# Hybrid attention/mLSTM block on one core: the low parts of the mixers' weight pieces and the rotary swap given to adding DMAs

## The chip, the cores and the metric

The kernel runs on one core of a Trainium2 chip. The metric is the device time of one execution in microseconds (us). Five engines matter: TensorE (PE in the profile, with its weight loads as PEld), VectorE (DVE), ScalarE (ACT), GpSimd (POOL) and SyncE (SP), which issues the loads from HBM.

## The reference, cut to what matters

Two layers, each a mixer and a convolutional feed-forward part, on 512 tokens of 1024 features, all in float32:

```
for l in range(2):
    mixed = hybrid_mixer(rms_norm(x), w_in[l], ..., w_out[l])    # attention heads | mLSTM heads
    x = x + rms_norm(mixed)
    ff = conv_ffn(rms_norm(x), w_up[l], ..., w_down[l])
    x = x + rms_norm(ff)

def apply_rotary(t):               # per head, 64 features
    t1, t2 = t[..., :32], t[..., 32:]
    return concatenate([t1 * cos - t2 * sin, t2 * cos + t1 * sin], axis=-1)
```

`hybrid_mixer` projects the normed input by `w_in` to queries and keys of the attention (rotated as above), values, the mLSTM's queries, keys and values, an output gate and the mLSTM's gates; it runs dilated window attention over 8 heads and an mLSTM in both directions over 4 heads, and multiplies the joined result by `w_out`.

## The kernel before, in words

**Precision.** Every weight tile and every activation is split in a high part (rounded to float32r) and a low part, the remainder. `mac` makes a product of three matmuls: high weight by high activation (line 230), low weight by high activation (231), high weight by low activation (232). The projection of values, in which the weights are the moving operand, does the same in lines 923 to 925.

**Pieces.** `plan` lists the weights in the order of use, in pieces of 128 x 1024 numbers (512 KB): per layer 28 of `w_in` (numbers 0 to 27 of the layer), 8 of `w_out`, 44 of `w_up` and 24 of `w_down`, 104 in all. SP loads a piece into one of three `wraw` buffers. `split_w` makes the parts: ScalarE copies the piece to `whi` (line 183), then VectorE subtracts that from the piece into `wlo` (`lo_part`, line 115), and the load of a later piece is issued, which waits until its `wraw` buffer is free. `whi` and `wlo` have three buffers each, so a piece can be split when the matmuls of the piece three before it are done. `prefetch` keeps two pieces split ahead of the one in use.

**The mixer's order.** `ORDER` names the pieces of four rounds: q and k are the mLSTM's projections, V the two pieces of the values (of both the mLSTM and the attention), a and b the attention's queries and keys of two heads. After the rounds come four pieces (m) of the output gate.

```
ORDER = ["qkaVb", "aqbkV", "qkVab", "qabkV"]
```

Between the steps of a projection the generators `attn` (stream A) and `mlstm` (stream M) are pumped: each `yield` in them ends one small share of work, and a rate says how many shares go with one step. The work of `attn(r)` is started when a, b and V of its round are done, and `A.run()` finishes it before the next a or b is rotated.

**The rotation.** `rot_out` takes the projection `ps` in PSUM (128 features: two heads of two halves of 32). Four ScalarE copies of 32 partitions (line 707) put the halves, swapped in pairs, into `b`; VectorE multiplies `ps` by the cosines (708), `b` by the sines with their signs (709) and adds (710). Then ScalarE and VectorE make high and low parts of the heads (lines 713 to 723 and `lo_part`).

**Who sets the order.** Every engine runs its own list in order. The lists are laid out by a planner from the program order, the dependences and its own estimates of how long each operation takes; an operation that the planner takes to be ready may stand ahead of one that comes earlier in the program.

Of the kernel before, what the change touches and what calls it, by code (L numbers as in the profile page):

```python
# [11 lines left out]
AF = mybir.ActivationFunctionType  # L12
ALU = mybir.AluOpType
# [12 lines left out]
RAW = 3  # L26
LINE = 256
RING = 3
HD = 128
KSC = HD ** -0.5  # L30
SUM1, ROW1, SUM2, ROW2 = [int(t * 2400) for t in (0.6, 3.3, 2, 8)]
# [50 lines left out]
def tile_hybrid_block(ctx: ExitStack, tc: tile.TileContext, xt, w_in, w_g, w_out, w_up, w_down, par, cst, out):  # L82
    nc = tc.nc
# [30 lines left out]
    def lo_part(dst, src, hi):  # L114
        nc.vector.tensor_tensor(out=dst, in0=src, in1=f32v(hi), op=ALU.subtract)  # L115
# [50 lines left out]
    def split_w(alloc=None):  # L166

        if not raw_q:
            return None
        raw, nk, i = raw_q.popleft()  # L170
        parts = {}
        n = 8
        k = 0
        while k < nk:
            if alloc is None:

                o = 16 if i in moving else 0
                hi, lo = (q.tile([P, 8 * P + LINE // 4], F32R, tag=t, name=t)[:, o:o + 8 * P].rearrange("p (k c) -> p k c", k=8)
                          for q, t in ((whi_p, "whi"), (wlo_p, "wlo")))
            else:  # L180
                hi, lo, n = alloc()
            m = min(n, nk - k)
            nc.scalar.copy(out=hi[:, 0:m, :], in_=raw[:, k:k + m, :])  # L183
            lo_part(lo[:, 0:m, :], raw[:, k:k + m, :], hi[:, 0:m, :])
            for j in range(m):
                parts[k + j] = (hi[:, j, :], lo[:, j, :])
            parts["all"] = (hi, lo)
            k += m
        load_raw()
        return parts  # L190
# [320 lines left out]
    def mixer(l, xp, first, mp, post):  # L511
# [7 lines left out]
        cosr, sinr, biasT, rowmask = cc("cos", T), cc("sin", T), cc("bias", 896), cc("rowmask", 8)  # L519
# [10 lines left out]
        gps, pss, scale, more = first  # L530
# [171 lines left out]
        def rot_out(ps, name):  # L702
            a = mp.tile([P, T], F32, tag="ca", bufs=2, name="ra")
            b = mp.tile([P, T], F32, tag="cu", bufs=2, name="rb")
            for q in range(4):
                o_ = 32 * (q ^ 1)
                nc.scalar.copy(out=b[32 * q:32 * q + 32, :], in_=ps[o_:o_ + 32, :])  # L707
            nc.vector.tensor_tensor(out=a, in0=ps, in1=cosr, op=ALU.mult)
            nc.vector.tensor_tensor(out=b, in0=b, in1=sinr, op=ALU.mult)
            nc.vector.tensor_tensor(out=a, in0=a, in1=b, op=ALU.add)  # L710
            A_, B_ = slice(0, 64), slice(64, 128)
            t = [mp.tile([P, T], F32R, tag=name + i, name=name + i) for i in "01"]
            nc.scalar.copy(out=t[0][A_], in_=a[A_])
            nc.scalar.copy(out=t[1][B_], in_=a[B_])
            if name == "aq":

                lo_part(t[0][B_], a[A_], t[0][A_])
                lo_part(t[1][A_], a[B_], t[1][B_])
                st[name] = t
            else:  # L720

                nc.scalar.copy(out=t[0][B_], in_=f32v(t[0][A_]))
                nc.scalar.copy(out=t[1][A_], in_=f32v(t[1][B_]))
                lo_part(klo[0][A_], a[A_], t[0][A_])
                lo_part(klo[1][B_], a[B_], t[1][B_])
                st[name] = (t, klo)
# [9 lines left out]
        def attn(hp):  # L736
            qs2, (kh, kl) = st["aq"], st["ak"]
            ct = new_cat(hp)

            def scores(a, qt):  # L740
                qs = slice(qt * P, (qt + 1) * P)
                s = s_ps()
                nc.tensor.matmul(out=s, lhsT=qs2[a][:, qs], rhs=kh[a], start=True, stop=False)  # L743
                nc.tensor.matmul(out=s, lhsT=qs2[a][:, qs], rhs=kl[a], start=False, stop=True)
                p_ = mp.tile([P, T], F32, tag="p", bufs=2, name="p")
                mx = sm.tile([P, 1], F32, tag="mx", bufs=4, name="mx")

                o_ = 384 - qt * P
                nc.vector.tensor_tensor_reduce(out=p_, in0=s, in1=biasT[:, o_:o_ + T], scale=-0.125, scalar=3e38,  # L749
                                               op0=ALU.add, op1=ALU.min, accum_out=mx)  # L750
                den = sm.tile([P, 1], F32, tag="den", bufs=4, name="den")
                nc.scalar.activation(out=p_, in_=p_, func=AF.Exp, scale=-1.0, bias=mx, accum_out=den)  # L752
                nc.vector.reciprocal(out=den, in_=den)
                nc.scalar.activation(out=p_, in_=p_, func=AF.Copy, scale=den)
                return p_

            def turn(p_, pt, qi):
                tp = t_ps()
                for kk in range(4):
                    nc.tensor.transpose(tp[:, kk * P:(kk + 1) * P], p_[:, kk * P:(kk + 1) * P], ident)  # L760
                tv = tp.rearrange("p (k q) -> p k q", k=4)
                hi = pt[0][:, :, qi * P:(qi + 1) * P]
                nc.scalar.copy(out=hi, in_=tv)
                lo_part(pt[1][:, :, qi * P:(qi + 1) * P], tv, hi)

            units = [(a, qt) for a in range(2) for qt in range(4)]
            held = scores(*units[0])
            yield
            for n, (a, qt) in enumerate(units):
                cur = held  # L770
                if n + 1 < len(units):
                    held = scores(*units[n + 1])
                    yield
                if qt % 2 == 0:
                    pt = (mp.tile([P, 4, 2 * P], F32R, tag="pth", bufs=2, name="pth"),
                          mp.tile([P, 4, 2 * P], F32R, tag="ptl", bufs=2, name="ptl"))
                turn(cur, pt, qt % 2)
                yield
                if qt % 2 == 1:
                    if qt == 1:  # L780
                        o = o_ps()
                    ov = o[:, (qt - 1) * P:(qt + 1) * P]
                    vs = st["av"]
                    for i in range(2):
                        for kk in range(4):
                            nc.tensor.matmul(out=ov, lhsT=vs[:, kk, a].rearrange("p i e -> p (i e)"), rhs=pt[i][:, kk, :],  # L786
                                             start=(i == 0 and kk == 0), stop=(i == 1 and kk == 3))
                    if qt == 3:
                        c = ct[64 * a:64 * a + 64, :]
                        nc.scalar.copy(out=c, in_=o[64:128, :])  # L790
                        nc.vector.tensor_tensor(out=c, in0=o[0:64, :], in1=c, op=ALU.add)
                    yield
# [96 lines left out]

        prefetch(RING - 1)  # L890
        scale_ready()
# [40 lines left out]
        for r in range(4):  # L932
            done = set()
            for c in ORDER[r]:
# [7 lines left out]
                else:  # L942
                    ps = proj()
# [10 lines left out]
        for r in range(4):  # L954
            ps = proj()
# [59 lines left out]
        for m in range(G, KT - 2):  # L1015
            w = take()
            ps = o_ps() if m == G else mm_ps()
# [167 lines left out]
def _constants():  # L1185
    import numpy as np

    f = np.float32
    c = np.zeros((P, NCC), f)

    def put(name, a):
        c[:, CC[name]:CC[name] + a.shape[1]] = a

    i = np.arange(P)
    put("ident", np.eye(P, dtype=f))
    put("tri_f", (i[:, None] <= i[None, :]).astype(f))
    put("tri_b", (i[:, None] >= i[None, :]).astype(f))
    put("mask_f", np.where(i[:, None] <= i[None, :], 0.0, -1e30).astype(f))
    put("mask_b", np.where(i[:, None] >= i[None, :], 0.0, -1e30).astype(f))
    rm = np.zeros((P, 8), f)  # L1200
    ic = np.zeros((P, 4), f)
    for part in range(4):
        for d in range(2):
            for j in range(4):
                for h in range(4):
                    r = part * 32 + d * 16 + j * 4 + h
                    rm[r, d * 4 + h] = 1.0
                    ic[r, j if d == 0 else 3 - j] = 1.0
    put("rowmask", rm)
    put("ind", ic)  # L1210
    put("dir", (i[:, None] // 16 % 2 == np.arange(2)).astype(f))
    dh = 64
    inv = (f(10000.0) ** (-np.arange(0, dh, 2, dtype=f) / f(dh))).astype(f)
    ang = np.arange(T, dtype=f)[:, None] * inv[None, :]
    cos, sin = np.cos(ang).astype(f).T, np.sin(ang).astype(f).T
    put("cos", np.concatenate([cos, cos, cos, cos]))
    put("sin", np.concatenate([-sin, sin, -sin, sin]))

    off = (np.arange(896)[None, :] - 384) - i[:, None]
    a = np.abs(off)  # L1220
    n = (a <= 64).astype(int) + ((a % 4 == 0) & (a <= 256)) + ((a % 16 == 0) & (a <= 1024))
    put("bias", np.where(n > 0, 8.0 * np.log(np.maximum(n, 1)), -1e30).astype(f))
    return c
# [58 lines left out]
```

## Time and profile before

| | |
|---|---|
| median of 3 runs | 1354.69 us (1354.68 to 1354.85) |
| the profiled execution | 1353.89 us, of which the span from the first to the last instruction is 1352.0 us |
| mean granted TensorE clock | 0.996 of full speed |
| busy, share of the span | TensorE 98%, VectorE 71%, ScalarE 53%, GpSimd 6% |
| DMA | 115.34 MB, mean 85 GB/s; the load queue takes 27.9% of the 16 DMA engines' time |

Stages in the profiled execution: the first mixer's projections and streams run from about 24 to 262 us, the second mixer's from about 695 to 931 us; between and behind them lie the products with `w_out` and the feed-forward parts. Shares of busy time are means over stages of different kinds; a matmul is shown from its start to its modelled end, which lies behind the start of the next one.

### The profile page before, as it was taken

Reading aid. Unit: us, or ns where it says so; the run is one execution under the profiler, and the core shown is the slowest. Engines: PE = TensorE matmul, PEld = TensorE weight load, DVE = VectorE, ACT = ScalarE, POOL = GpSimd, SP = SyncE. Lnnn points to the kernel's source line nnn. Section 1 sums busy time; section 2 is a strip of 40 time slices with the busy share of each in tenths; the row PEclk is TensorE's granted clock in tenths of the full one; section 3 lists DMA queues with packets and bytes.
Section 4 is the critical chain, followed back from the end, with each engine's and each line's share of the span. In section 5 each row is a group of like instructions: output and inputs, shape, how many; then the busy total and the mean of one; then the engine's idle time right before and its main releaser. Section 6 shows DMA issues by size and latency. Waiting matters only on the chain.

```text
span 1352.0 us, 18666 instructions
## 1 busy us (share of the span) xinstructions
PE 1323.9 (98%) x7152; PEld 1128.6 (83%) x7152; DVE 954.0 (71%) x1901; ACT 713.1 (53%) x1218; POOL 85.3 (6%) x100
## 2 busy tenths in 40 slices
PE   7999999999999999999989999999999999999996
PEld 5888878899888888888978898888998888888886
DVE  6999798847887777422499988887569777773233
ACT  5686696654544444323347867966446444443220
POOL 0000000024000000001130000000320000000002
PEclk9999999999999999999999999999999999999998
DMA  6212112231233332333321122123213333333321
GB/s 238 63 41 86 47 48 79 78 126 44 68 107 96 104 97 90 90 97 111 96 85 51 60 64 65 45 79 99 90 47 96 106 95 94 94 96 96 98 86 63
DMA packets 34089, 115.34 MB, mean 85 GB/s; under 512 B 3664, under 2 KB 6352, under 8 KB 34000
## 3 DMA queue, kind: packets, MB, share of 16 engines
q1 hardware_dynamic: 34000, 114.15, 27.9%
q8 instruction: 56, 0.92, 0.3%
q14 instruction: 33, 0.27, 0.1%
HBM read 112.04 MB, written 2.10 MB: 84 GB/s over the span
## 4 chain that ended last, share of the span: by engine, by line
PE 85%; DVE 7%; ACT 7%; issue 1%; DMA 0%; POOL 0%; SPq 0%; ACTq 0%; DVEq 0%
PE mm L230 18%; PE mm L232 18%; PE mm L231 18%; PE o L230 5%; PE o L231 5%; PE o L232 5%; PE mm L924 2%; PE mm L925 2%; PE mm L923 2%; PE o L786 2%; ACT rb L707 1%; PE t L760 1%; PE t L344 1%; DVE wlo L115 1%; ACT p L752 1%; PE s L743 1%
## 5 line engine op out<-in xcount | busy, mean ns | idle before, releaser
L115 DVE TENSOR_TENSOR wlo<-wraw,whi 128x1024 fp32r<-128x1024 f32 (+1 forms) x192 | 236.5, 1234 | 175.4 <-ACT whi L183 173.3
L230 PE MATMUL mm<-ah,whi 128*128 128x512 f32 (+1 forms) x880 | 337.0, 383 | 0.0
L232 PE MATMUL mm<-al,whi 128*128 128x512 f32 (+1 forms) x880 | 333.2, 380 | 0.8 <-DVE al L378 0.7
L231 PE MATMUL mm<-ah,wlo 128*128 128x512 f32 (+1 forms) x880 | 333.3, 379 | 0.0
L183 ACT CAST whi<-wraw 128x1024 fp32r<-128x1024 f32 (+1 forms) x192 | 198.0, 1035 | 163.2 <-PE mm L232 112.3
L232 PEld LDWEIGHTS mm<-al,whi 128*128 128x128 f32 x880 | 166.2, 189 | 30.8 <-DVE al L378 1.6
L230 PEld LDWEIGHTS mm<-ah,whi 128*128 128x128 f32 x880 | 166.5, 189 | 28.8 <-ACT whi L183 0.5
L231 PEld LDWEIGHTS mm<-ah,wlo 128*128 128x128 f32 x880 | 166.6, 189 | 27.3
L326 POOL TENSOR_TENSOR acc<-acc,sq 128x512 f32<-128x512 f32 x22 | 29.5, 1342 | 1127.0 <-ACT sq L323 1122.6
L230 PE MATMUL mm<-hh,whi 128*128 128x512 f32 x220 | 85.6, 389 | 0.0
L231 PE MATMUL mm<-hh,wlo 128*128 128x512 f32 x220 | 85.6, 389 | 0.0
L232 PE MATMUL mm<-hl,whi 128*128 128x512 f32 x220 | 85.6, 389 | 0.0
L1059 DVE TENSOR_TENSOR u<-mm,prow 128x512 f32<-128x512 f32 x64 | 43.8, 687 | 50.0 <-PE mm L232 39.6
L1076 ACT CAST hh<-cv 128x512 fp32r<-128x512 f32 x44 | 27.3, 620 | 87.6 <-DVE cv L1073 87.6
L923 PE MATMUL mm<-whi,ah 128*128 128x256 f32 x256 | 72.4, 284 | 0.9 <-DVE cu L664 0.9
L924 PE MATMUL mm<-wlo,ah 128*128 128x256 f32 x256 | 71.7, 280 | 0.4 <-DVE wlo L115 0.4
L925 PE MATMUL mm<-whi,al 128*128 128x256 f32 x256 | 71.4, 279 | 0.0
L1071 ACT ACTIVATE cg<-cg 128x512 f32<-128x512 f32 x44 | 27.8, 632 | 74.6 <-DVE cg L1065 74.3
L231 PE MATMUL o<-ah,wlo 128*128 128x512 f32 (+1 forms) x160 | 60.6, 379 | 0.0
L232 PE MATMUL o<-al,whi 128*128 128x512 f32 (+1 forms) x160 | 60.5, 378 | 0.0
L230 PE MATMUL o<-ah,whi 128*128 128x512 f32 (+1 forms) x160 | 60.5, 378 | 0.0
L752 ACT ACTIVATE p<-p,mx 128x512 f32<-128x512 f32 x64 | 46.2, 722 | 18.2 <-DVE mx L749 16.9
(319 smaller groups left out, 2754.9 us busy)
## 6 DMA issues: line engine op xcount, KB each, us to landing
wraw<-in_w_up SPq DMA_DIRECT2D x88, 512.0 KB, 3.6
wraw<-in_w_in SPq DMA_DIRECT2D x56, 512.0 KB, 3.6
wraw<-in_w_down SPq DMA_DIRECT2D x32, 512.0 KB, 3.5
wraw<-in_w_out SPq DMA_DIRECT2D x16, 512.0 KB, 3.6
wraw<-in_w_down SPq DMA_DIRECT2D x16, 384.0 KB, 3.1
x<-in_xt SPq DMA_DIRECT2D x4, 512.0 KB, 7.3
out_dram<-x SPq DMA_DIRECT2D x8, 256.0 KB, 2.1
tb<-in_cst SPq DMA_DIRECT2D x2, 967.0 KB, 5.4
```

The source lines that it names most:

```text
L115: nc.vector.tensor_tensor(out=dst, in0=src, in1=f32v(hi), op=ALU.subtract)
L183: nc.scalar.copy(out=hi[:, 0:m, :], in_=raw[:, k:k + m, :])
L230: nc.tensor.matmul(out=ps, lhsT=hi, rhs=rh, start=first, stop=False)
L231: nc.tensor.matmul(out=ps, lhsT=lo, rhs=rh, start=False, stop=False)
L232: clock[1] = nc.tensor.matmul(out=ps, lhsT=hi, rhs=rl, start=False, stop=last).ins
L326: e.tensor_tensor(out=self.acc[:, cols], in0=self.acc[:, cols], in1=sq, op=ALU.add)
L752: nc.scalar.activation(out=p_, in_=p_, func=AF.Exp, scale=-1.0, bias=mx, accum_out=den)
L923: nc.tensor.matmul(out=o_, lhsT=xh, rhs=hi, start=(k == 0), stop=False)
L924: nc.tensor.matmul(out=o_, lhsT=xh, rhs=lo, start=False, stop=False)
L925: clock[1] = nc.tensor.matmul(out=o_, lhsT=xl, rhs=hi, start=False, stop=(k == KT - 1)).ins
L1059: nc.vector.tensor_tensor(out=u, in0=ps, in1=st["row"], op=ALU.mult)
L1071: nc.scalar.activation(out=g, in_=g, func=AF.Gelu_apprx_tanh)
```

## The change

Three things are changed. In pieces 4 to 27 of layer 0 and 0 to 27 of layer 1 (52 pieces) the low part is no longer made by VectorE: a second pass of ScalarE writes the piece times -1.0 into `wlo`, rounded as `whi` is, and a DMA issued by GpSimd adds the piece to it, which leaves the remainder. In `rot_out`, VectorE multiplies `ps` by cosines and by sines straight from PSUM, and four DMAs of GpSimd add the 32-partition quarters of the second product, swapped in pairs, onto the first; the signs of the sine table are swapped to fit. And `attn` begins with two empty shares.

```diff
+PIECES = 104
@@ split_w
             nc.scalar.copy(out=hi[:, 0:m, :], in_=raw[:, k:k + m, :])
-            lo_part(lo[:, 0:m, :], raw[:, k:k + m, :], hi[:, 0:m, :])
+            if alloc is None and i % PIECES < 28 and i > 3:
+
+                nc.scalar.activation(out=lo[:, 0:m, :], in_=raw[:, k:k + m, :], func=AF.Copy, scale=-1.0)
+                nc.gpsimd.dma_start(out=lo[:, 0:m, :], in_=raw[:, k:k + m, :], accum_op=ALU.add)
+            else:
+                lo_part(lo[:, 0:m, :], raw[:, k:k + m, :], hi[:, 0:m, :])
@@ rot_out
+            nc.vector.tensor_tensor(out=a, in0=ps, in1=cosr, op=ALU.mult)
+            nc.vector.tensor_tensor(out=b, in0=ps, in1=sinr, op=ALU.mult)
+
             for q in range(4):
                 o_ = 32 * (q ^ 1)
-                nc.scalar.copy(out=b[32 * q:32 * q + 32, :], in_=ps[o_:o_ + 32, :])
-            nc.vector.tensor_tensor(out=a, in0=ps, in1=cosr, op=ALU.mult)
-            nc.vector.tensor_tensor(out=b, in0=b, in1=sinr, op=ALU.mult)
-            nc.vector.tensor_tensor(out=a, in0=a, in1=b, op=ALU.add)
+                nc.gpsimd.dma_start(out=a[32 * q:32 * q + 32, :], in_=b[o_:o_ + 32, :], accum_op=ALU.add)
@@ attn
             units = [(a, qt) for a in range(2) for qt in range(4)]
+            for _ in range(2):
+                yield
             held = scores(*units[0])
@@ _constants
-    put("sin", np.concatenate([-sin, sin, -sin, sin]))
+    put("sin", np.concatenate([sin, -sin, sin, -sin]))
```

## Rows read from the trace of the kernel before

**Rows 1.** The page: busy time, share of the span and instructions of each engine.

```profile
PE 1323.9 (98%) x7152; PEld 1128.6 (83%) x7152; DVE 954.0 (71%) x1901; ACT 713.1 (53%) x1218; POOL 85.3 (6%) x100
```

**Rows 2.** Stretches: length, busy PE, PEld, DVE, ACT, POOL; granted clock; DMA share, GB/s.

```profile
24.00:262.00 238.00, 234.92 (x1436) 202.16 (x1436) 211.80 (x535) 172.77 (x340) 0.13 (x1) 1.00 0.21 63
262.00:672.00 410.00, 409.24 (x2039) 348.02 (x2038) 246.28 (x372) 172.94 (x247) 31.59 (x31) 1.00 0.32 95
695.00:931.00 236.00, 233.46 (x1433) 200.83 (x1431) 211.07 (x529) 173.20 (x341) 0.00 (x0) 1.00 0.22 64
...
60.00:100.00 40.00, 38.26 (x232) 32.37 (x231) 37.46 (x97) 35.20 (x70) 0.13 (x1) 1.00 0.13 40
170.00:205.00 35.00, 34.36 (x192) 27.75 (x191) 31.48 (x87) 32.68 (x67) 0.00 (x0) 1.00 0.16 47
```

**Rows 3.** Waits of TensorE's weight loads, first mixer, then second: us, times, longest.

```profile
PEld t L760 <- ACT p L754: 2.4, 8, 0.4
...
PEld s L864 <- DVE hs L874: 0.2, 1, 0.2
...
PEld t L760 <- ACT p L754: 2.8, 9, 0.4
...
PEld o L817 <- DVE kw L808: 0.2, 1, 0.2
```

**Rows 4.** Costliest groups by line in the first mixer: busy us, mean ns, idle before.

```profile
L115 DVE TENSOR_TENSOR wlo<-wraw,whi 128x1024 fp32r<-128x1024 f32 x28 | 34.2, 1221 | 3.4 <-ACT whi L183 3.3
...
L183 ACT CAST whi<-wraw 128x1024 fp32r<-128x1024 f32 x28 | 29.1, 1046 | 9.1 <-PE mm L925 4.8 <-PE mm L232 4.2
L752 ACT ACTIVATE p<-p,mx 128x512 f32<-128x512 f32 x32 | 23.1, 722 | 7.5 <-DVE mx L749 6.9 <-DVE den L753 0.5
L754 ACT ACTIVATE p<-p,den 128x512 f32<-128x512 f32 x32 | 22.7, 718 | 1.7 <-DVE den L753 1.6
L707 ACT COPY rb<-mm 32x512 f32<-32x512 f32 x32 | 18.5, 577 | 3.6 <-PE mm L232 3.1
```

**Rows 5.** DMA issues: size and median us from issue to landing.

```profile
wraw<-in_w_in SPq DMA_DIRECT2D x56, 512.0 KB, 3.6
x<-in_xt SPq DMA_DIRECT2D x4, 512.0 KB, 7.3
graw<-in_w_g SPq DMA_DIRECT2D x2, 64.0 KB, 3.6
```

**Rows 6.** Timeline around the second V piece of round 1: start, us, engine.

```profile
91.75 2.00 ACT L183 CAST whi<-wraw 128x1024 fp32r<-128x1024 f32 x2
...
97.78 1.22 DVE L115 TENSOR_TENSOR wlo<-wraw,whi 128x1024 fp32r<-128x1024 f32 x1
...
99.05 0.39 PE L924 MATMUL mm<-wlo,ah 128*128 128x256 f32 x1 [0.20 <-DVE wlo L115]
```

**Rows 7.** Timeline around the second V piece of round 3.

```profile
201.53 1.05 ACT L183 CAST whi<-wraw 128x1024 fp32r<-128x1024 f32 x1
...
202.75 1.22 DVE L115 TENSOR_TENSOR wlo<-wraw,whi 128x1024 fp32r<-128x1024 f32 x1
...
202.20 0.28 PE L924 MATMUL mm<-wlo,ah 128*128 128x256 f32 x1
...
205.62 0.28 PE L924 MATMUL mm<-wlo,ah 128*128 128x256 f32 x1
```

**Rows 8.** Timeline of the rotation of round 0's b, to the first scores.

```profile
50.32 2.34 ACT L707 COPY rb<-mm 32x512 f32<-32x512 f32 x4 [1.02 <-PE mm L232]
...
56.81 0.69 DVE L710 TENSOR_TENSOR ra<-ra,rb 128x512 f32<-128x512 f32 x1
...
57.54 0.63 ACT L713 CAST ak<-ra 64x512 fp32r<-64x512 f32 x1 [3.49 <-DVE ra L710]
...
59.55 0.39 PE L232 MATMUL mm<-al,whi 128*128 128x512 f32 x1
59.78 0.39 PE L743 MATMUL s<-ak,aq 128*128 128x512 f32 x1
```

## The prediction

> **What bounds the kernel now.** I read the page first: TensorE is busy for 1323.9 of 1352.0 us [rows 1], so a change that takes no matmul away can only win what TensorE waits. The second view is the busy time by stretch. Between the mixers TensorE idles 0.76 of 410 us, in the first mixer 3.08 of 238, in the second 2.54 of 236 [rows 2]: 5.6 us in the two places that the change touches, which is a lower bound. In the timeline a 512-column matmul is shown 0.39 us long, but the next one starts after 0.23 us (59.55 to 59.78) [rows 8], so each wait may hide another 0.16 us. The third view, the waits of the weight loads, has 23 rows with 41 waits in the first mixer and 22 rows with 37 in the second [rows 3]; 78 waits by 0.16 us give 12.5 us, and the upper bound 18.1. I take the lower bound and half of the rest, some 12 us. That is the whole purse.
>
> Whose are these 12 us? Of the 14.0 us that the 23 rows add up to, 5.0 end with VectorE's work (with 1.5 of a kind that names no releaser, and stands before the mLSTM's products of W, which wait for VectorE's results); of the 13.1 us of the other 22, 4.1. That is about a third, 4 of the 12 us. Another third stands behind ScalarE's softmax and transposed scores (the first row of each mixer alone is 2.4 and 2.8 us) [rows 3], and part of that is VectorE's again: ScalarE itself idles 6.9 us in the first mixer for the maxima that VectorE makes [rows 4]. VectorE is the crowded engine: 211.8 of 238 us, 89%, and 94% from 60 to 100 us. ScalarE is at 172.8 us, 73%, but in two stretches it is as full as VectorE: 35.2 of 40 us and 32.7 of 35 [rows 2].
>
> **The change part by part.** *VectorE.* 52 low parts by 1.221 us [rows 4] are 63.5 us, 16 additions by 0.69 [rows 8] are 11.0: 74.5 us less. The other two multiplications stay. Over the two mixers (474 us) VectorE goes from 422.9 us to about 348, from 89% to 73%.
>
> *ScalarE.* The 64 quarter copies by 0.577 go, 36.9 us. 52 negated passes come. No such row exists; the plain pass over 1024 columns takes 1.046 us, and a copy with a scale at 512 columns takes 0.718 where a plain one takes 0.577 [rows 4], so a pass costs 1.05 to 1.30. I take 1.05, the row of the same width: 54.6 us. Net 17.7 us more, from 73% to 77%. In the two full stretches three or four passes come and about eight copies go, so these get no fuller.
>
> *GpSimd and the DMA engines.* GpSimd has 0.13 us of work in the mixers [rows 2]. It gets 52 DMAs of 512 KB and 64 of 64 KB, 31.5 MB in all. The mixers' DMA share is 0.21 to 0.22 now; at the rate of the loads it would about double. What one adding DMA takes from issue to landing no row shows. A 512 KB load lands in 3.6 us and the slowest of that size in 7.3; a 64 KB one in 3.6 [rows 5]. These are the two ends for the low part. I take 5.0, nearer to the load in undisturbed traffic, which is the same bytes at the same quiet share of the DMA engines, but above it, because the sum must read its target too; and 3.6 for a quarter. What GpSimd needs to issue one is counted in the landing.
>
> The Trainium skill, in Collectives: The Full Stack (The bandwidth ceiling: the fold count and why AG ≠ RS ≠ AR), says that an add in the DMA path is slow not through its arithmetic but because it needs two source reads; with the rate and the fixed 2.0 us that DMA: Bandwidth & Descriptors (Anatomy of one DMA) gives, its estimate would be 4.4 us in place of 3.2 for a copy. No run here shows it yet; by it the third round's piece below would be 2.4 us late instead of 3.0 and the rival of the late low parts would lose some of its chance.
>
> *Where the later low part meets its reader.* The chain was high part, then VectorE's 1.22 us after its queue. It becomes negated pass 1.05 (behind the high part on ScalarE), then 5.0: about 6 us. In the timeline I went through the 28 pieces of each mixer, from the end of the high part to the first matmul that reads the low part. Clearly shorter than 6 us it is only for the second V piece of rounds 1 and 3, whose high part is made late. In round 1 its high part ends at about 92.8 (the first of two), VectorE's queue brings the low part only at 99.0, and TensorE is shown waiting 0.20 us for it [rows 6]: the new chain ends at 92.8 + 1.05 + 5.0 = 98.9, no later than now. In round 3 it ends at 202.6 and is read at 205.6 [rows 7]; the new one ends at 208.6, 3.0 us late in both layers. What covers it: in a V step the four blocks of tokens need the first V piece for half of their matmuls, 48 of 0.12 us each (half of 0.23, half the columns), 5.6 us, of which only 12 stand ahead of that read; 4.2 us can be drawn forward. In round 1 the planner has done just that: the low part comes 6.2 us behind its high part, and TensorE idles 0.20 us for it [rows 6]. So I price it at 0.5 us a layer; with the cover gone it is 3.0 a layer.
>
> *The rotation.* Before, from the end of b's matmuls at 50.3 to ScalarE's first head part at 57.5 pass 7.2 us, of which 2.34 are the quarter copies and 0.69 the addition; the rest is VectorE's queue [rows 8]. The four DMAs come in the place of these 3.0 us and take 3.6 from the last issue, so the heads come at the same time within 1 us, earlier if VectorE's queue is shorter. Behind them stand ScalarE's copies of the head parts, and behind these the scores, at 59.8 now. The two empty shares put the scores some steps later in the program, and where V follows b (rounds 1 and 3) they are not near. I price it at 0, bounds -2 and +1 at each of the four places (rounds 0 and 2, two layers).
>
> *The sum.* VectorE's 4 us of waits: 3 go. ScalarE's 4 us: 2 go, because the maxima come sooner, and the added passes put none back. The V pieces cost 1. In all 4.0 us less. The profiled execution would come from 1353.89 to 1349.9; it ran 0.8 below the median, so against the median 1354.69 I predict **1350.7 us**.
>
> **The rivals.** 0.2% is 2.7 us, about what a measurement of this kernel can tell from no change.
>
> *The relief is hidden.* ScalarE, 77% full and in chains with VectorE at every softmax step, becomes the engine that the same waits end with. For it: the waits that open both lists already end with ScalarE [rows 3]. Against it: where it is fullest, the copies that go outweigh the passes. Gain 2 in place of 5, minus 1: 1353.7.
>
> *The low parts land late.* Place: the second V piece of rounds 1 and 3. Price: with a landing of 7.3 us, round 3's is 202.6 + 1.05 + 7.3 - 205.6 = 5.3 us late, round 1's 101.2 - 99.1 = 2.1, in two layers 14.8 in all, less the 5 of relief: 1364.5 if nothing covers it; with the cover of 4.2 in round 3, 6.4 in all and 1356.1. The middle is 1360. For it: TensorE's list is fixed, so a landing that the planner puts too low is not covered. Against it: the slack of all other pieces. It decides, a loss of 5 + 2.7 us, from a landing of 5.5 us on without the cover and of 7.6 with it.
>
> *The quarters go one behind another.* Then a rotation costs 4 x 3.6 = 14.4 us in place of 3.0, the scores of rounds 0 and 2 come 11 us later, and with some half of that covered by other projections the four places cost about 20 us: 1370. DMA: Bandwidth & Descriptors of the Trainium skill (Rules for kernel authors) says that two transfers to disjoint partition halves serialize on the same 16 engines. For it: all four share one issuer. Against it: 64 KB are a small part of what lands in the same 3.6 us as 512 KB [rows 5], so most of the time is latency, which overlaps.
>
> **How the numbers follow.** The forecast 0.50 (its own range 1346 to 1352), hidden 0.26, late low parts 0.15, quarters in a row 0.09. The first is faster, the second the same, the last two slower. Below 1346 would need 9 of the 12 us, 0.06; above 1359 lie nearly all of the last rival and a third of the one before, 0.13. So 1346 to 1359.
>
> **What would show it.** In the profile after, VectorE should be near 880 us and ScalarE near 731 in all; VectorE's share of the first mixer near 73%; TensorE's idle in the two mixers below 5.6 us; the DMA issues should show a 512 KB adding DMA below 5.5 us and the quarters below 5. Wrong would be: long waits of TensorE for the low part at a V step, waits for `ak` or `aq` in front of line 743 that end with a DMA, ScalarE standing at lines 713 and 714.

## The result, and the profile after

The changed kernel takes 1383.23 us (median of 4 runs, 1382.76 to 1386.14) against 1354.77 on the same chip: a ratio of 1.0214, 95% interval 1.02 to 1.0228, some 29 us slower. The prediction was 1350.7. Of three kernels below one execution each lies far above its fellows (1878.97, 1641.5 and 4683.68 us) and is left out of the times given; the first is the profiled one of the rotary alone, so that trace is not used.

The page of the changed kernel, busy time and the chain that ended last (compare [rows 1]):

```profile
PE 1329.8 (96%) x7152; PEld 1134.6 (82%) x7152; DVE 894.6 (65%) x1833; ACT 723.9 (52%) x1206; POOL 183.2 (13%) x216
...
PE 79%; DVE 7%; DMA 6%; ACT 4%; issue 3%; POOL 1%; SPq 0%; ACTq 0%; POOLq 0%; DVEq 0%
```

VectorE's work shrank by 59.4 us and ScalarE's grew by 10.8, much as they were meant to, and the span still grew from 1352.0 to 1381.0 us. A DMA now holds 6% of the chain; the page puts 5% of the span on `ra<-rb`, the rotary's quarters. The same stretches as in [rows 2], with the columns named there:

```profile
24.00:262.00 238.00, 224.06 (x1363) 193.29 (x1363) 172.74 (x468) 167.09 (x309) 47.27 (x57) 0.99 0.54 120
262.00:672.00 410.00, 408.94 (x2002) 346.11 (x2000) 248.41 (x385) 182.17 (x267) 32.50 (x32) 1.00 0.34 98
710.00:945.00 235.00, 221.17 (x1333) 190.43 (x1334) 170.25 (x453) 165.94 (x307) 47.81 (x57) 0.98 0.56 124
```

Between the mixers TensorE is as busy as before. In each mixer TensorE now stands about 14 us (238 - 224.06, 235 - 221.17), against 3.1 and 2.5. What it waits for in the first mixer (us in total, times, longest; compare [rows 3]):

```profile
PEld s L749 <- ACT ak L728: 6.5, 2, 3.3
PEld t L766 <- ACT p L760: 6.5, 10, 3.7
PEld t L893 <- DVE hs L889: 2.6, 1, 2.6
PEld mm L932 <- DMA wlo<-wraw: 2.3, 3, 0.9
```

Of these rows only the last names a DMA: these are the V pieces. The first is the scores waiting for a head. The largest single wait, 3.7 us, is a transpose waiting for a softmax share (`p`), which does not use the rotation it stands behind. The DMA issues (compare [rows 5]):

```profile
wraw<-in_w_in SPq DMA_DIRECT2D x56, 512.0 KB, 4.2
wlo<-wraw POOLq DMA_DIRECT2D x52, 512.0 KB, 5.3
...
ra<-rb POOLq DMA_DIRECT2D x64, 64.0 KB, 4.7
```

How one late landing spreads is seen in the timeline of round 2's a in the changed kernel (start us, us, engine; in brackets the idle time before and what ended it):

```profile
164.20 0.19 ACT L758 ACTIVATION_READ_ACCUMULATOR p<-p,mx 128x1 f32 x1
168.16 0.62 ACT L719 CAST aq<-ra 64x512 fp32r<-64x512 f32 x1 [3.77 <-DMA ra<-rb]
168.68 0.72 ACT L760 ACTIVATE p<-p,den 128x512 f32<-128x512 f32 x1
...
164.43 0.16 DVE L759 RECIPROCAL den<-den 128x1 f32<-128x1 f32 x1
168.81 0.68 DVE L116 TENSOR_TENSOR aq<-ra,aq 64x512 fp32r<-64x512 f32 x1 [4.22 <-ACT aq L719]
...
165.79 0.39 PE L237 MATMUL mm<-ah,wlo 128*128 128x512 f32 x1
169.46 1.05 PE L766 MATMUL t<-c,p 128*128 128x128 f32 x4 [3.28 <-ACT p L760]
...
159.59 0.87 POOL L188 DMA_DIRECT2D wlo<-wraw  x1 [2.96 <-ACT wlo L187]
160.23 3.46 POOL L716 DMA_DIRECT2D ra<-rb  x4
```

`den` is ready at 164.6, so the softmax share `p` (L760) could run at once. But ScalarE's list has the cast of a head (L719) ahead of it, and that cast waits for quarters that were issued at 160.23 behind a 512 KB low part. ScalarE stands 3.77 us, VectorE 4.22 us behind ScalarE, TensorE 3.28 us behind both. In the whole execution ScalarE stands 28.7 us, in 14 places, for quarters that have not landed.

Behind this wait TensorE's granted clock fell too. The windows of the same place, and the start of the second layer's mixer (columns as in [rows 2]):

```profile
160.00:168.00 8.00, 6.17 (x40) 4.93 (x38) 4.27 (x9) 2.49 (x6) 3.69 (x5) 1.00 0.95 220
168.00:176.00 8.00, 6.54 (x35) 6.02 (x36) 5.26 (x9) 4.81 (x10) 0.00 (x0) 0.79 0.22 66
...
712.00:720.00 8.00, 6.99 (x23) 5.09 (x22) 6.97 (x13) 3.08 (x6) 0.88 (x1) 0.57 0.94 195
```

The granted clock is 0.79 in the 8 us behind the wait, a mean of the levels 2.4 and 1.2 GHz. In the two mixers there are four such windows (0.82, 0.79, 0.57, 0.79) and one of 0.97; 8 x (0.18 + 0.21 + 0.43 + 0.21 + 0.03) = 8.5 us is what they may have cost at most, since TensorE stands in part of them. In the kernel before, the clock is 1.00 in both mixers [rows 2].

### The profile page after: what moved, and what is told of

It reads as the page before. It is cut to its first block, busy times and chain, and to the rows that moved or that the text cites. A ratio compares the mean times of both kernels' runs of the same rounds, so it can differ in the third digit from the quotient of the medians.

```text
span 1381.0 us, 18850 instructions
## 1 busy us (share of the span) xinstructions
PE 1329.8 (96%) x7152; PEld 1134.6 (82%) x7152; DVE 894.6 (65%) x1833; ACT 723.9 (52%) x1206; POOL 183.2 (13%) x216
## 4 chain that ended last, share of the span: by engine, by line
PE 79%; DVE 7%; DMA 6%; ACT 4%; issue 3%; POOL 1%; SPq 0%; ACTq 0%; POOLq 0%; DVEq 0%
PE mm L236 17%; PE mm L237 17%; PE mm L238 17%; PE o L236 5%; PE o L238 5%; PE o L237 5%; DMA ra<-rb 5%; PE t L766 1%; PE o L794 1%; PE mm L932 1%; PE mm L933 1%; PE mm L931 1%; PE t L350 1%; PE s L749 1%; DVE ca L677 1%
## 5 line engine op out<-in xcount | busy, mean ns | idle before, releaser
L116 DVE TENSOR_TENSOR wlo<-wraw,whi 128x1024 fp32r<-128x1024 f32 x140 | 172.9, 1239 | 159.3 <-ACT whi L184 157.5
L188 POOL DMA_DIRECT2D wlo<-wraw x52 | 50.8, 977 | 307.4 <-ACT wlo L187 209.8
L187 ACT ACTIVATE wlo<-wraw 128x1024 fp32r<-128x1024 f32 x52 | 55.0, 1058 | 30.9 <-PE mm L237 17.3
L716 POOL DMA_DIRECT2D ra<-rb x64 | 53.0, 1342 | 67.0 <-DVE rb L712 29.1
```

The source lines that it names most:

```text
L187: nc.scalar.activation(out=lo[:, 0:m, :], in_=raw[:, k:k + m, :], func=AF.Copy, scale=-1.0)
L188: nc.gpsimd.dma_start(out=lo[:, 0:m, :], in_=raw[:, k:k + m, :], accum_op=ALU.add)
L716: nc.gpsimd.dma_start(out=a[32 * q:32 * q + 32, :], in_=b[o_:o_ + 32, :], accum_op=ALU.add)
```

## The experiments

Differences in us are (ratio - 1) x 1354.8, from the ratio to the kernel before on the same chip; the intervals are 95%. Line numbers in a fence are those of the kernel it is from.

### One part at a time

**Low parts only.** Rotation, sine row and shares as before; of the change this hunk:

```diff
+            if alloc is None and i % PIECES < 28 and i > 3:
+                nc.scalar.activation(out=lo[:, 0:m, :], in_=raw[:, k:k + m, :], func=AF.Copy, scale=-1.0)
+                nc.gpsimd.dma_start(out=lo[:, 0:m, :], in_=raw[:, k:k + m, :], accum_op=ALU.add)
+            else:
+                lo_part(lo[:, 0:m, :], raw[:, k:k + m, :], hi[:, 0:m, :])
```

> Only the low parts of the 52 mixer pieces go to ScalarE and the adding DMA; the rotation is as before, with no empty shares. Theory A (the quarters of the rotation land 5 to 11 us after VectorE's product, ScalarE's list stands behind the casts that wait for them, and that is most of the 28.5 us): 1355 to 1361 us, TensorE's waits for wlo about 3 us in all. Rival B (the low parts themselves, late or by the order that the planner makes of them, are most of it): 1370 us or more.

Measured: 1369.34 us, ratio 1.0113 (1.0096 to 1.013), +15.3.

**Rotary only.** The other hunks; the low parts as before.

```diff
-                nc.scalar.copy(out=b[32 * q:32 * q + 32, :], in_=ps[o_:o_ + 32, :])
+                nc.gpsimd.dma_start(out=a[32 * q:32 * q + 32, :], in_=b[o_:o_ + 32, :], accum_op=ALU.add)
...
+            for _ in range(2):
+                yield
```

> Only the rotation by adding DMAs, with the two empty shares; all low parts on VectorE as before. Theory A: 1368 to 1380 us, with 2 to 4 us waits of TensorE at the first scores and the transposes of rounds 0 and 2. Rival B: 1355 to 1362. Rival C (the quarters are late only because they queue behind a 512 KB low part in GpSimd's queue, so that neither part alone costs much): both this and the low parts alone stay under 1362.

Measured: 1364.79 us, ratio 1.0078 (1.0061 to 1.0095), +10.6. The runs further down show the same edits in parts.

**The change without the empty shares, and the empty shares alone.**

```diff
-            for _ in range(2):
-                yield
```

> The changed kernel without the two empty shares in the attention stream. If the shares only make room for the late heads: 1383 to 1390 us, later than or equal to the changed kernel. If they cost more than they cover, since they push shares into the part of the stream that runs without cover: 1376 to 1381.

> The kernel before with nothing but the two empty shares. Theory A expects them to cost little: 1354 to 1357 us. A rival that lays the loss on the shares expects 1362 or more.

Measured: 1380.06 us, 1.018 (1.016 to 1.02) without them; 1354.82 us, 1.0000 (0.9991 to 1.0009) with nothing but them. They cost nothing alone. In the changed kernel they may cost something: without them it is 24.4 us over, with them 29.0, and the two intervals meet at 1.02. The waits of TensorE's weight loads over the whole execution, without the shares and then with them:

```profile
PEld s L749 <- ACT ak L728: 14.6, 4, 4.5
PEld t L766 <- ACT p L760: 3.8, 12, 0.5
```

```profile
PEld t L766 <- ACT p L760: 13.2, 16, 3.9
PEld s L749 <- ACT ak L728: 9.6, 4, 3.3
```

The shares took 5.0 us off the scores' wait for a head and put 9.4 on the transposes' wait for softmax shares.

So each of the two parts is slower by itself: 15.3 + 10.6 = 25.9 (the two shares are in the rotary's 10.6), and 3 us more come when they are together.

### The low parts

**Not at the second V pieces** (pieces 4, 11, 15 and 23 of a layer, one for each round).

```diff
-            if alloc is None and i % PIECES < 28 and i > 3:
+            if alloc is None and i % PIECES < 28 and i > 3 and i % PIECES not in (4, 11, 15, 23):
```

> Low parts alone, but the second V piece of every round (numbers 4, 11, 15, 23) stays on VectorE. In the run with all low parts TensorE waits 10.3 us for the adding DMA of those pieces (three in the first mixer, two in the second). Theory A2 (those waits, the start of layer 1 and nothing else): 1358 to 1361 us, 10 less. Rival (the waits only move, as the passes on ScalarE and the order are the cause): 1365 or more.

Measured: 1359.63 us, 1.0036 (1.0022 to 1.005), +4.9. Four pieces of 28 carry 15.3 - 4.9 = 10.4 of the 15.3 us. In the run with low parts only, round 1's piece looks like this (ScalarE, GpSimd, TensorE; the last two rows are round 3's piece in the first and in the second layer):

```profile
93.95 1.04 ACT L184 CAST whi<-wraw 128x1024 fp32r<-128x1024 f32 x1
95.21 1.04 ACT L187 ACTIVATE wlo<-wraw 128x1024 fp32r<-128x1024 f32 x1
...
96.67 0.88 POOL L188 DMA_DIRECT2D wlo<-wraw  x1 [15.30 <-PE mm L238]
...
101.19 0.39 PE L930 MATMUL mm<-wlo,ah 128*128 128x256 f32 x1 [1.60 <-DMA wlo<-wraw]
...
212.49 0.39 PE L930 MATMUL mm<-wlo,ah 128*128 128x256 f32 x1 [2.76 <-DMA wlo<-wraw]
...
890.98 0.39 PE L930 MATMUL mm<-wlo,ah 128*128 128x256 f32 x1 [2.70 <-DMA wlo<-wraw]
```

High part done at 95.0, negated pass at 96.25, read at 101.19 after a wait of 1.60 that ends with the landing: 6.1 us behind the high part, as the prediction had it (1.05 + 5.0). Round 3's piece keeps TensorE waiting 2.76 and 2.70 us.

**Not at the start of layer 1** (numbers 107 and 108 of the plan).

```diff
+            if alloc is None and i % PIECES < 28 and i > 3 and i not in (107, 108):
```

> Low parts alone, but the two V pieces at the start of layer 1 (numbers 3 and 4 there) stay on VectorE. Theory A2: at the start of layer 1 the negated passes stand in ScalarE's list in front of the copy of the gate scores (gs), whose PSUM buffer the next projection needs; without them the start costs 4 to 5 us less: 1364 to 1365.5. Rival (that start is slower because VectorE's short steps come in another order): 1368 to 1370.

Measured: 1366.51 us, 1.009 (1.0073 to 1.0107), +12.2, so 3.1 us of the 15.3. Number 108 is also the second V piece of round 0 in layer 1, so the 3.1 and the 10.4 overlap. The place is shown with the passes without the landing, below.

**Only pieces with a long slack** (38 pieces).

```diff
+            if alloc is None and i % PIECES < 28 and i % PIECES > 4 and i % PIECES not in (6, 11, 15, 23):
```

> Low parts alone, only pieces that had 9 us or more from high part to reader: not 0 to 4, 6, 11, 15, 23 of either layer, 38 pieces in all. Theory A2: no wait for an adding DMA is left, no pass stands at the start, VectorE is relieved of some 46 us: 1351 to 1355, at least level with the kernel before. Rival (ScalarE's passes cost in themselves): 1357 to 1362.

Measured: 1357.35 us, 1.0021 (1.0012 to 1.0031), +2.8. No wait of TensorE ends with an adding DMA now, and VectorE is relieved of 38 passes, yet nothing is gained. The issue and the traffic of 38 of the 52 DMAs, with their passes, cost these 2.8 us at most, since the relief itself is worth nothing (below).

**The relief alone.**

```diff
-                nc.scalar.activation(out=lo[:, 0:m, :], in_=raw[:, k:k + m, :], func=AF.Copy, scale=-1.0)
-                nc.gpsimd.dma_start(out=lo[:, 0:m, :], in_=raw[:, k:k + m, :], accum_op=ALU.add)
+                lo = hi
```

> Left out: the low parts of 52 pieces of W; their matmuls read the high part a second time, so VectorE is spared 63.5 us of work and neither ScalarE nor GpSimd gets any in its place. Theory A (the prediction's purse: 3 to 5 us of TensorE's waits end with VectorE): 1349.5 to 1351.5. Theory B (VectorE's fullness costs nothing that can be had back, the waits move to the next releaser): 1353.5 to 1355.5. Theory A also expects VectorE's waits of TensorE in the mixers to go to about a quarter.

Measured: 1355.31 us, 1.0006 (0.9997 to 1.0015). Theory A falls: 52 passes off VectorE are worth nothing. One place where it went is the gates' chain of round 0 (the short steps from the mLSTM's gates to `lf` and on), in the kernel before and in this one:

```profile
50.94 0.19 DVE L577 SCALAR_TENSOR_TENSOR lf<-gp,fg 128x32 f32<-128x32 f32 x1
51.19 0.39 PE L581 MATMUL t<-lf,tri 128*128 128x16 f32 x2 [0.23 <-DVE lf L577]
```

```profile
46.31 0.19 DVE L582 SCALAR_TENSOR_TENSOR lf<-gp,fg 128x32 f32<-128x32 f32 x1
46.56 0.40 PE L586 MATMUL t<-lf,tri 128*128 128x16 f32 x2 [0.95 <-DVE lf L582]
```

VectorE delivers `lf` 4.6 us sooner, and TensorE's list asks for it 4.6 us sooner and waits longer, 0.95 us for 0.23. These lines fit lists that the planner lays out for the new work: what comes free early is read early, and the projections that it overtakes are still to be done. The weight loads' waits that end with VectorE add up to 4.3 and 4.4 us in the two mixers, where the kernel before has 3.5 and 2.8: they did not fall. The transposes of `hs` in round 0 moved in the same way, from 111.97 without a wait to 106.26 with 0.62.

**The passes without the landing.**

```diff
                 nc.scalar.activation(out=lo[:, 0:m, :], in_=raw[:, k:k + m, :], func=AF.Copy, scale=-1.0)
-                nc.gpsimd.dma_start(out=lo[:, 0:m, :], in_=raw[:, k:k + m, :], accum_op=ALU.add)
```

> Left out: the adding DMAs of the 52 low parts; the negated pass alone writes what the matmuls read. So VectorE is relieved, ScalarE has its 55 us of passes, and nothing lands late. If the passes stand in front of what the softmax and the start of the second layer wait for (my reading of the runs so far): 1357 to 1361, with some 3 to 5 us of it at the start of layer 1, and 9 or 10 us below the kernel with the DMAs. If only the late landing costs anything: 1351 to 1355.

Measured: 1362.25 us, 1.0055 (1.0042 to 1.0067), +7.5. The passes cost 7.5 - 0.8 = 6.7 us over the relief alone, the adding DMAs (issue, traffic and landing) another 15.3 - 7.5 = 7.8. The start of layer 1 in this kernel, ScalarE and then TensorE:

```profile
699.80 1.05 ACT L187 ACTIVATE wlo<-wraw 128x1024 fp32r<-128x1024 f32 x1
700.76 0.36 ACT L399 COPY prow<-s 128x256 f32<-128x256 f32 x1
701.01 0.57 ACT L548 COPY gs<-mm 32x512 f32<-32x512 f32 x1
...
699.94 0.68 PE L364 MATMUL s<-ident_rs,rs_y 128*128 128x128 f32 x4 [1.91 <-DVE rs_y L301]
701.64 0.50 PE L235 MATMUL mm<-ah,whi 128*128 128x512 f32 x1 [1.02 <-ACT gs L548]
```

And with VectorE's low parts left at that place, ScalarE alone:

```profile
700.15 0.57 ACT L549 COPY gs<-mm 32x512 f32<-32x512 f32 x1 [0.68 <-PE mm L492]
700.63 1.04 ACT L184 CAST whi<-wraw 128x1024 fp32r<-128x1024 f32 x1
```

`gs` is the copy that frees the PSUM tile that the next projection needs. Here it stands first, and in the kernel before too (695.29). With the passes two high parts, two negated passes and two row copies come ahead of it (from 696.70 on; the fence has the last two rows of them), so TensorE has no projection with which to fill the 1.91 us of the norm's chain.

### The rotary

**The heads' casts on GpSimd**, so that ScalarE's list has no wait for a quarter.

```diff
-            nc.scalar.copy(out=t[0][A_], in_=a[A_])
-            nc.scalar.copy(out=t[1][B_], in_=a[B_])
+            nc.gpsimd.tensor_copy(out=t[0][A_], in_=a[A_])
+            nc.gpsimd.tensor_copy(out=t[1][B_], in_=a[B_])
```

> Rotation by adding DMAs and the empty shares, low parts on VectorE, but the head parts' copies (lines 713 to 723) are made by GpSimd, so that ScalarE's list has nothing in it that waits for the quarters. If ScalarE standing in front of the casts is what costs: 1356 to 1361 us in place of 1366. If the heads simply come too late for the scores: 1366 or more, since GpSimd's copies are not faster.

Measured: 1372.35 us, 1.0131 (1.0114 to 1.0147), +17.7. This is no proof that the heads are simply late: VectorE's low parts of the heads now wait for GpSimd's casts (8.7 us for `aq` and 7.1 for `ak` behind the first casts, by the waits of VectorE), and the rest of VectorE's list stands behind them. GpSimd's first casts mostly take 0.61 us, as ScalarE's 0.62 do; its copies within `ak` take 1.35 and 1.01 on average.

**Rounds 1 and 3 only; rounds 0 and 2 only.** In the other rounds the copies as before, with a subtraction.

```diff
+            if hp % 2:
...
+            else:
+                for q in range(4):
+                    o_ = 32 * (q ^ 1)
+                    nc.scalar.copy(out=b[32 * q:32 * q + 32, :], in_=ps[o_:o_ + 32, :])
...
+                nc.vector.tensor_tensor(out=a, in0=a, in1=b, op=ALU.subtract)
```

> Rotation by the adding DMAs in rounds 1 and 3 only, in rounds 0 and 2 the copies as before (with a subtraction, because the sign of the sine row is the new one). If the rotary's loss of 11 us sits where scores follow b directly (rounds 0 and 2): 1354 to 1357. If it comes from ScalarE's list that stands behind a cast that waits for the quarters, wherever that is, half of the loss stays: 1359 to 1362.

> Rotation by the adding DMAs in rounds 0 and 2 only, by copies in rounds 1 and 3. If the places add up: the rotary alone was 11 us over, rounds 1 and 3 alone 2 us under, so rounds 0 and 2 should be 12 to 15 us over, 1367 to 1370. If the loss of the rotary alone comes from the number of DMAs rather than their place, half of it: 1359 to 1361.

Measured: 1351.95 us, 0.9983 (0.9974 to 0.9991), -2.3; and 1367.76 us, 1.0102 (1.0085 to 1.0119), +13.8. The sum, 11.5, is the rotary's 10.6 within the intervals, so the whole loss sits in rounds 0 and 2, and in rounds 1 and 3 the quarters are a gain. The quarters land in 3.2 us (median) in the one and in 4.5 in the other, and ScalarE stands 4.0 us for them (3 times) in the one and 21.7 (10 times) in the other. The first head of round 0 with the quarters there (GpSimd, ScalarE, VectorE, TensorE):

```profile
42.30 3.30 POOL L711 DMA_DIRECT2D ra<-rb  x4 [39.53 <-DVE fg L576]
...
49.02 0.62 ACT L721 CAST aq<-ra 64x512 fp32r<-64x512 f32 x1 [2.89 <-DMA ra<-rb]
...
49.67 0.69 DVE L116 TENSOR_TENSOR aq<-ra,aq 64x512 fp32r<-64x512 f32 x1 [2.73 <-ACT aq L721]
...
53.50 0.19 DVE L578 SCALAR_TENSOR_TENSOR lf<-gp,fg 128x32 f32<-128x32 f32 x1
...
53.75 0.61 PE L582 MATMUL t<-lf,tri 128*128 128x16 f32 x2 [3.01 <-DVE lf L578]
54.19 0.59 PE L583 MATMUL t<-lf,tri 128*128 128x16 f32 x2
```

In the kernel before, the same cast:

```profile
44.38 0.62 ACT L713 CAST aq<-ra 64x512 fp32r<-64x512 f32 x1
```

At this place it is the head a, not b, and not the scores: from the first issue to the cast pass 6.7 us, the cast comes 4.6 us later than before, VectorE stands 2.73, and the gates' chain behind it comes 2.6 us later (`lf` at 53.50, not 50.94). The last rows fit a lower clock as well (0.82 granted from 48 to 56 us): the small matmuls start 0.44 us apart, where before they started 0.24 apart (51.19 and 51.43). In round 0 of the second layer it is b:

```profile
739.82 0.62 ACT L721 CAST ak<-ra 64x512 fp32r<-64x512 f32 x1 [8.74 <-DMA ra<-rb]
...
740.47 0.68 DVE L116 TENSOR_TENSOR klo<-ra,ak 64x512 fp32r<-64x512 f32 x1 [2.86 <-ACT ak L721]
...
742.13 1.25 PE L827 MATMUL o<-v,kw 128*128 128x129 f32 x6 [2.04 <-DVE kw L818]
```

Here too TensorE waits for the mLSTM's chain in VectorE's list behind the head (`kw`), not for the scores. The scores wait 3.1 us for `ak` in this whole run.

**Six empty shares in place of two; heads put 6 us later.** Both with the rotary alone, the second with the six shares too.

```diff
-            for _ in range(2):
+            for _ in range(6):
...
+            def casts():
...
+            later(int(6.0 * 2400), casts)
```

> The rotary alone, with six empty shares ahead of the first scores in place of two, so that some 3 us more of projection work stand between b and the scores. If the scores' own wait for the heads is the loss, 1357 to 1361 (each of four places gives back 1 to 3 us). If ScalarE's list behind the casts is the loss, or the time comes back at the end of the attention that now ends later, 1364 to 1368.

> As the rotary alone with six empty shares, but the casts and low parts of the heads are put into the program 6 us of projection work behind the issue of the quarters, so that neither ScalarE's nor VectorE's list has a head part at its top while the quarters are under way. If the loss is other work that stands behind the head parts in these two lists (softmax shares, the gates' chain): 1353 to 1359. If the loss is that the attention ends later, or lies in the DMAs themselves: 1363 to 1368, as with the six shares.

Measured: 1365.56 us, 1.0083 (1.007 to 1.0097), +11.2; and 1372.84 us, 1.0128 (1.0113 to 1.0143), +17.3. More distance to the scores gives nothing back. With the six shares TensorE has no wait left that ends with `ak`, but the transposes wait 9.9 us for softmax shares, where the kernel before has 5.1, and the time is the same: in the rotary alone the scores were not the place. The second didn't do what it was made for, since the list asks for the heads where it did before:

```profile
49.14 0.62 ACT L721 CAST aq<-ra 64x512 fp32r<-64x512 f32 x1 [2.94 <-DMA ra<-rb]
...
49.79 0.69 DVE L116 TENSOR_TENSOR aq<-ra,aq 64x512 fp32r<-64x512 f32 x1 [2.79 <-ACT aq L721]
```

So it says nothing about the standing. Its transposes wait 14.3 us for softmax shares; why it is slower still stays open.

**Quarters that nobody waits for.**

```diff
-                nc.gpsimd.dma_start(out=a[32 * q:32 * q + 32, :], in_=b[o_:o_ + 32, :], accum_op=ALU.add)
+                nc.gpsimd.dma_start(out=aside[32 * q:32 * q + 32, :], in_=b[o_:o_ + 32, :], accum_op=ALU.add)
```

> The rotary alone, with the 64 quarter DMAs issued and landed as before but added into a tile that nobody reads: the heads are cast from the cosine product alone, so the rotated half is left out of the result. The issues on GpSimd, the traffic and the two multiplications stay; only the wait for the landing goes. If the loss of 11 us is that ScalarE and VectorE stand in front of head parts until the quarters land: 1350 to 1355. If it is the traffic, the issuing or the place of the scores: 1363 to 1367.

> The changed kernel without either wait for a landing: the low parts are the negated pass alone (52 adding DMAs left out), the quarters add into a tile that nobody reads. What stays is ScalarE's 55 us of passes, the issues of the quarters and the new order. If the landings are the rest of the loss: the 8 us that the passes cost by themselves, less what the rotation without its copies gives, 1355 to 1362. If the two parts have a cost together that is not a landing: above 1366.

Measured: 1348.64 us, 0.9954 (0.9942 to 0.9967), -6.2, for the rotary; 1354.44 us, 0.9996 (0.9987 to 1.0005), -0.5, for the changed kernel with such quarters and without the 52 adding DMAs of the low parts. The first stretch of each, first the rotary:

```profile
24.00:262.00 238.00, 236.40 (x1456) 205.01 (x1457) 209.38 (x537) 157.25 (x311) 25.48 (x33) 1.00 0.31 75
```

```profile
24.00:262.00 238.00, 236.40 (x1454) 203.76 (x1454) 186.26 (x513) 176.31 (x335) 25.49 (x33) 1.00 0.30 74
```

GpSimd still issues the 32 quarters in each mixer (25.5 us) and the bytes still move; TensorE is busier than in the kernel before. The quarters' traffic and issue cost nothing that shows. The wait, from the product to the landing, is 10.6 + 6.2 = 16.8 us of the rotary. These heads are cast from the first product alone, so a part of the 16.8 is that they come sooner than in any full rotation (the first at 40.85, before at 44.38), and the lists may be laid out otherwise. Without the low parts' DMAs as well, the changed kernel is level with the kernel before: the two together are its whole loss, 29.0 + 0.5.

### Looking for a better version

**VectorE multiplies the four quarters itself**, in all rounds, and in rounds 0 and 2 with the DMAs in 1 and 3.

```diff
-                nc.scalar.copy(out=b[32 * q:32 * q + 32, :], in_=ps[o_:o_ + 32, :])
+                nc.vector.tensor_tensor(out=b[32 * q:32 * q + 32, :], in0=ps[o_:o_ + 32, :], in1=sinr[32 * q:32 * q + 32, :], op=ALU.mult)
```

> The kernel before with one edit: VectorE multiplies the four quarters straight from the other quarter of the PSUM tile by the sine (four instructions of 32 partitions), so ScalarE's 64 quarter copies go and VectorE gets three short multiplications more per rotation, some 33 us in all if each takes as long as the full one. If ScalarE's copies and the chain through them are what costs, and VectorE's load costs little (63 us off it brought nothing): 1349 to 1353. If VectorE at 95% and more becomes the bound: 1357 to 1365.

> Rounds 1 and 3 by the adding DMAs, as in the run that was 2 us under the kernel before, rounds 0 and 2 by VectorE's quarters in place of ScalarE's copies. If both gains add up: 1348 to 1351. If VectorE becomes the bound in rounds 0 and 2: 1353 to 1358.

Measured: 1376.92 us, 1.0168 (1.0155 to 1.0182), +22.8; and 1360.76 us, 1.0047 (1.0035 to 1.006), +6.4. A quarter takes VectorE 687 ns, as long as a whole tile, 44.0 us in all, and it is busy 219.12 of the first 238 us. So VectorE's load is not free, though its relief is worth nothing. The clock has a share in it: in the profiled execution (1380.84 us, the slowest of the five) six 8 us windows of the mixers have a granted clock of 0.62 to 0.80, which is 11.4 us at most. The best version found is the one with the quarters in rounds 1 and 3 alone, 2.3 us under the kernel before.

## Why the prediction was wrong

In us over the kernel before, by the runs above: relief of VectorE +0.8 (nothing); ScalarE's passes +6.7; the low parts' adding DMAs +7.8; the rotation without its copies and without a wait -6.2; the wait for the quarters +16.8; both parts together 3 more. That is 29. These are differences of whole kernels, each with lists of its own, so what another order gives or takes is counted with them.

- *The purse.* At least half of it was there: the rotary without a wait, which leaves the swapped half out of the heads, took 6.2 of the 12 us. The busy times were roughly right too: VectorE came to 894.6 us where 880 was expected, ScalarE to 723.9 for 731. The 52 low parts took 50 us off VectorE (954.0 to 904.0 in the relief alone), not 63.5, in part at least because neighbours overlap: in the kernel before, a low part is shown from 39.84 us for 1.22, and the next row starts at 40.97.
- *"VectorE's 4 us of waits: 3 go."* This step failed. I took waits that end with VectorE for waits that VectorE's fullness makes. In the relief alone the readers shown moved up with the work, and the waits stayed: the rows that name VectorE add up to 8.7 us in the two mixers, 6.3 before.
- *"The added passes put none back."* This failed too. I compared copies and passes in the two full stretches of the mixers and didn't look at the start of layer 1, where there are no copies to go and `gs` stands behind the passes: 3.1 us with the DMAs of the two pieces.
- *The second V pieces, 0.5 us a layer with cover.* The chain of 6 us behind the high part was right, and rounds 1 and 3 were places of it; the cover was not there. In the run with low parts only TensorE waited 2.76 and 2.70 us in round 3, where I had 3.0 without the cover, and 1.60 in round 1, where I had nothing; a wait of 0.83 in round 0 I had not seen. The second V pieces of all four rounds are worth 10.4 us in the two layers, passes included, where I had 1. My own price without the cover, 6 us, was nearer.
- *The rotation, priced at 0 with bounds of -2 and +1.* This is the step that decided: 10.6 us alone, a wait of 16.8 less a gain of 6.2. Two things were wrong in it. I had the heads at the same time within 1 us; the first of round 0 came 4.6 us later. Four quarters take 6.7 us from the first issue to the cast, 7.9 behind a low part, where I had 3.6 from the last issue: GpSimd spends 0.8 us on each issue, which I had counted in the landing, and the landing takes 4.5 in rounds 0 and 2. And I asked only who reads the heads, the scores. I had named "ScalarE standing at lines 713 and 714" as what would be wrong without pricing it. What stands behind the casts in ScalarE's list, and behind their low parts in VectorE's, is the softmax and the gates' chain, and TensorE waits for these. The scores do wait as well, 9.6 us in the changed kernel, but a larger distance to them moved the wait and won no time.
- *The price of a wait.* I counted a wait at its length. In four windows of 8 us the granted clock was 0.57 to 0.82, with a fifth of 0.97 at most 8.5 us in the changed kernel, where the kernel before had 1.00 in both mixers [rows 2].
- *The rivals.* The late low parts (1356 to 1364.5) came true as a mechanism, at 7.8 us of adding DMAs. "The quarters go one behind another" had the time nearest to the result, 1370, by a mechanism that is not what happened: four in a row would have been 14.4 us, and 6.7 were measured. The hidden relief (1353.7) is nearest to what the relief alone showed (no gain, 1355.31), for another reason than the one given: ScalarE got no work there, and the lines shown moved in the order.

The Trainium skill, in TensorE: Matmul & The Clock Gate (Architectural detail: the array is 16× 32×32, not 1× 128×128), says that the queues of ScalarE and VectorE are strictly first in, first out. The trace agrees: 3.77 us of ScalarE in front of one cast, with a share behind it whose input was ready. That is the rule that I should have priced.

The Trainium skill, in Collectives: The Full Stack (The bandwidth ceiling: the fold count and why AG ≠ RS ≠ AR), had led, with the rate that the prediction names, to an estimate of 4.4 us for an adding DMA of 512 KB. The trace has 4.9 with the low parts only and 5.3 in the changed kernel; the measurement decides.

Open: why VectorE's four short products cost 22.8 us when 50 us off it bring nothing (the clock, a PSUM tile held longer and the queue all fit); why the deferred heads were slower than the six shares; where the other 3.6 us of the passes go, beyond the start of layer 1 (the scores wait 4.1 us for `ak` with the passes alone, 2.6 in the relief alone); what makes the 3 us of both parts together, for which the quarters' place behind a low part in GpSimd's queue and the empty shares both fit; why the quarters land later in rounds 0 and 2.

## What to carry to other kernels

When work moves to an asynchronous path, price the instruction that waits for it by everything behind it in its engine's list, not only by the reader of its result: here giving the readers of the heads more distance won nothing, and the wait for the quarters cost 17 us. Relief of a crowded engine was worth nothing here, where the order of the bottleneck's list was laid out anew around it; test it first by leaving the work out. Use such a DMA only where nothing near it waits, as in rounds 1 and 3, and put no pass ahead of a copy that frees the buffer the bottleneck needs next.

## What the hardware showed that I had not expected

- Adding DMAs from SBUF to SBUF: 512 KB landed in 5.3 us (median of 52; 4.9 with the low parts only), 64 KB quarters in 3.2 us in rounds 1 and 3 alone and in the rotary that nobody waits for, in 4.5 in rounds 0 and 2 alone and in 4.7 in the changed kernel. GpSimd was busy 0.98 us for each of the large ones (50.8 us for 52) and 0.83 for a quarter (53.0 us for 64).
- After a TensorE wait of 3.3 us the granted clock was 0.79 over the next 8 us.
- On VectorE 32 partitions by 512 take 687 ns, no less than 128 by 512 (0.69, [rows 8]).
